# A hybrid recurrent decoder layer on one core: another centring for the layernorms, sums on VectorE, rows of 548 floats, and an alternating third merge

## The chip, the cores and the metric

The kernel runs on one core of a Trainium2 chip. Five engines work in parallel and each takes its own instructions in a fixed order: TensorE (PE in the profile; its weight loads are PEld), VectorE (DVE), ScalarE (ACT), GpSimd (POOL) and SyncE (SP), which here issues the loads of the weights. The metric is the device time of one execution in microseconds (us).

## The reference

One layer of a decoder is applied to 512 prompt tokens and to 8 x 4 sample tokens, 544 in all, with a model width of 1024:

```
proj   = x @ w_in + b_in
h_gla, h_ml, h_hg = three token mixers of parts of proj
gates  = sigmoid(mg).reshape(..., 3, 1024)
merged = gates[0]*(h_gla @ w_up_gla) + gates[1]*(h_ml @ w_up_ml) + gates[2]*(h_hg @ w_up_hg)
x = layernorm(alpha*x + merged @ w_out, ln1_g, ln1_b)
hid = square(relu(x @ w_ff_up))
x = layernorm(alpha*x + hid @ w_ff_down, ln2_g, ln2_b)
```

Outputs are x and the states of the mixers. All numbers are float32.

## The kernel before

Activations are held transposed: channels on the 128 partitions, the 544 tokens along a row, eight tiles of 128 channels (KD). A product of full precision is made of three: each operand is split into a high part and a rest (xh and xl of x, wh and wl of a weight tile), and high x high, high x rest and rest x high are summed. A gemm (L163) of one output tile with eight input tiles is therefore 8 x 3 x 2 = 48 matmuls, since the 544 tokens go in two halves of 272.

Weights come by `wload` (L133): a DMA into one of three buffers raw, ScalarE copies it into wh (L141), VectorE subtracts to get wl (L142). wh and wl have two buffers each, so the weights of a gemm can be split only when the gemm before the last has read its own. The PSUM results have two buffers too, and one is free again when VectorE has read it.

The stages follow one another: input projection and the three mixers, with gemms of the projection filling TensorE; three merges; output projection with the first layernorm; the FFN in two blocks of 16 hidden tiles; the second layernorm. Inside an engine a scheduler fixes the order at build time; `high_priority` draws weight splits and evacuations forward.

A **merge** (class at L839) takes a branch: `gates` computes four gate tiles (a gemm over x, L853 to add the bias, L206 to L208 for the sigmoid), `split` divides the branch's result into hh and hl, `products` makes four tiles of h @ w_up, multiplies them by their gates (L868) and adds them to `merged` on GpSimd (L872). The third merge, of the HGRN2 branch, has two input tiles, so that a product has 12 matmuls; it computes all eight gates first, then all eight products, and splits each finished tile of merged into mh and ml (L179, L180).

The **first layernorm** works on tiles as they leave the output projection (L1015 to L1020; L1019 adds alpha*x). `ln_tile` (L953) adds up tiles 0 to 3, takes the mean over those 512 channels by a matmul with ones5 (L967), and centres: tiles 0 to 3 in one go, later tiles as they come (L972). Of each centred tile ScalarE takes the square (L974), and GpSimd adds tile and square to the sums a1 and a2 (L978, L979); for the last tile VectorE does. `put_x1` (L1009) writes the FFN's operands x1h and x1l. `ln_sums` and `ln_end` turn the sums into ne (the negative mean) and rstd. The **second layernorm** uses the same `ln_tile` on six tiles (L1061); tiles 6 and 7 are treated in token halves at the end (L1077 to L1095), with their weights split into lh and ll (L1071). Then each half gets ne added, rstd multiplied and the affine step (L1096 to L1107). The lists ADDP, MULP and AFFD (L30) say which tiles GpSimd adds, GpSimd multiplies and VectorE scales; the rest is VectorE's and ScalarE's.

The operands xh, xl, x1h and x1l are tiles of [128, 8, TX] with TX = T + 2 = 546 floats per row; the two extra columns hold the layernorm's gain and bias for the first FFN gemms.

## Time and profile before

| | us |
|---|---|
| median of 3 runs | 968.91 |
| lowest and highest run | 965.64 and 971.26 |
| the profiled execution | 968.76 |
| its span, first to last instruction | 966.9 |
| mean granted TensorE clock over the span | 0.977 of full speed |

A row of the profile names the line, the engine, the operation, and what it writes and reads (`out<-in`, buffer numbers left out); x is a count. A wait is put down to the instruction that ended it. The granted clock is the share of TensorE's full clock that it was allowed to run at. Busy time of TensorE contains waiting inside its pipeline, so that the start-to-start distance of matmuls says more than the length of one record.

### The profile page before, as it was taken

To read this page: it belongs to the slowest core of one execution; us is meant where nothing else is said; L and a number is where in the kernel's file an instruction comes from. 1 tells how busy PE (TensorE), PEld (TensorE's weight loads), DVE (VectorE), ACT (ScalarE), POOL (GpSimd) and SP (SyncE) were. 2 spreads that over 40 slices of the span, in tenths; PEclk is the share of its full clock that TensorE was granted. 3 is DMA by queue.
4 is the path that set the end of the run, shared out by engine and by line. 5 is a ranking of instruction groups with operands and counts; after the bars stand their busy time and mean duration, and the time that the engine had idled before them with its cause. 6 is when DMAs were issued, how large, how long until landed. Compare 5 with 4: busy or idle time off the path is not lost.

```text
span 966.9 us, 17405 instructions
## 1 busy us (share of the span) xinstructions
PE 926.0 (96%) x7279; PEld 910.7 (94%) x7279; DVE 569.1 (59%) x877; ACT 404.5 (42%) x688; POOL 232.9 (24%) x210
## 2 busy tenths in 40 slices
PE   8999999799999999999989798999999999999795
PEld 7998999799999999999989798999999999999794
DVE  4895467866775676773565855553222455532836
ACT  4386223643555443545523356542111344521414
POOL 0311232643102435120235692000000000001722
PEclk9999999899999999999999899999999999999898
DMA  7321241022132112041144222222222222222202
GB/s 258 118 86 44 84 129 57 16 87 88 60 96 90 49 47 97 25 158 55 33 154 121 79 67 87 88 88 88 87 88 87 88 87 88 88 87 88 85 3 93
DMA packets 37598, 82.73 MB, mean 86 GB/s; under 512 B 12709, under 2 KB 18341, under 8 KB 37521
## 3 DMA queue, kind: packets, MB, share of 16 engines
q1 hardware_dynamic: 25072, 73.28, 23.3%
q10 hardware_dynamic: 12384, 8.33, 3.0%
q8 instruction: 57, 0.93, 0.4%
q14 instruction: 21, 0.16, 0.1%
q0 software_dynamic: 64, 0.02, 0.0%
HBM read 76.51 MB, written 5.09 MB: 84 GB/s over the span
## 4 chain that ended last, share of the span: by engine, by line
PE 86%; DVE 6%; POOL 3%; issue 2%; ACT 1%; DMA 1%; ACTq 0%; DVEq 0%
PE g L158 74%; PE g L83 3%; PE lv L401 2%; POOL merged L1050 2%; POOL merged L1049 1%; DVE wl L142 1%; DVE qe L393 1%; DVE merged L972 1%; PE o L458 1%; DVE x1l L1013 1%; PE oTm L760 1%; PE qkp L673 0%; PE oT L282 0%; DVE ml L180 0%; DMA fw<-in_wfirst 0%
## 5 line engine op out<-in xcount | busy, mean ns | idle before, releaser
L142 DVE TENSOR_TENSOR wl<-raw,wh 128x1024 fp32r<-128x1024 f32 (+2 forms) x139 | 168.4, 1212 | 152.4 <-ACT wh L141 149.6
L141 ACT ACTIVATE wh<-raw 128x1024 fp32r<-128x1024 f32 (+2 forms) x139 | 133.3, 959 | 277.0 <-PE g L158 258.8
L158 PE MATMUL g<-xh,wh 128*128 128x272 f32 x752 | 162.1, 295 | 0.0
L158 PE MATMUL g<-xh,wl 128*128 128x272 f32 x752 | 161.2, 293 | 0.0
L158 PE MATMUL g<-xl,wh 128*128 128x272 f32 x752 | 161.1, 294 | 0.0
L158 PEld LDWEIGHTS g<-xl,wh 128*128 128x128 f32 x752 | 120.8, 191 | 0.9 <-issue 0.5
L158 PEld LDWEIGHTS g<-xh,wh 128*128 128x128 f32 x752 | 121.0, 192 | 0.7 <-issue 0.2
L158 PEld LDWEIGHTS g<-xh,wl 128*128 128x128 f32 x752 | 121.1, 192 | 0.3
L158 PE MATMUL g<-x1h,wh 128*128 128x272 f32 (+1 forms) x512 | 107.1, 290 | 2.9 <-DVE relu L1036 2.9
L158 PE MATMUL g<-x1l,wh 128*128 128x272 f32 (+1 forms) x512 | 106.9, 290 | 0.0
L158 PE MATMUL g<-x1h,wl 128*128 128x272 f32 (+1 forms) x512 | 106.9, 290 | 0.0
L158 PEld LDWEIGHTS g<-x1h,wh 128*128 128x128 f32 x512 | 81.2, 189 | 3.3 <-DVE relu L1036 3.3
L158 PEld LDWEIGHTS g<-x1l,wh 128*128 128x128 f32 x512 | 81.5, 190 | 0.1
L158 PEld LDWEIGHTS g<-x1h,wl 128*128 128x128 f32 x512 | 80.8, 188 | 0.0
L961 POOL TENSOR_TENSOR a<-merged 128x544 f32<-128x544 f32 x2 | 4.8, 2421 | 295.6 <-ACT wh L141 284.3
L158 PE MATMUL g<-hidl,wh 128*128 128x272 f32 x280 | 58.1, 289 | 0.0
L158 PE MATMUL g<-hidh,wh 128*128 128x272 f32 x280 | 57.9, 288 | 0.0
L158 PE MATMUL g<-hidh,wl 128*128 128x272 f32 x280 | 57.8, 288 | 0.0
L1038 ACT ACTIVATE relu<-relu,gw 128x544 f32<-128x544 f32 x32 | 24.0, 750 | 77.2 <-DVE relu L1037 77.2
L872 POOL TENSOR_TENSOR merged<-merged,gb 128x544 f32<-128x544 f32 x16 | 26.8, 1678 | 86.8 <-ACT gb L207 47.8
L215 DVE TENSOR_SCALAR gb<-g,vec 128x544 f32<-128x544 f32 x24 | 18.8, 782 | 45.2 <-PE g L158 45.1
L158 PEld LDWEIGHTS g<-hidl,wh 128*128 128x128 f32 x280 | 44.0, 188 | 0.0
(405 smaller groups left out, 1863.3 us busy)
## 6 DMA issues: line engine op xcount, KB each, us to landing
raw<-in_wff SPq DMA_DIRECT2D x64, 512.0 KB, 3.6
raw<-in_win SPq DMA_DIRECT2D x47, 512.0 KB, 3.2
xr<-in_xT SPq DMA_DIRECT2D x16, 272.0 KB, 3.2
raw<-in_wout SPq DMA_DIRECT2D x8, 512.0 KB, 4.0
out_yT<-merged SPq DMA_DIRECT2D x8, 272.0 KB, 2.4
fw<-in_wfirst ACTq DMA_DIRECT2D x8, 256.0 KB, 5.4
raw<-in_wup_ml SPq DMA_DIRECT2D x8, 192.0 KB, 2.3
raw<-in_wup_gla SPq DMA_DIRECT2D x8, 192.0 KB, 2.4
```

The costliest lines, as they stand in the source:

```text
L83: nc.tensor.matmul(first_ps[i][hf], w[:, i * 128:(i + 1) * 128], a[:, k, hf * HT:(hf + 1) * HT], start=(k == 0 and n == 0), stop=(k == KD ...
L141: nc.scalar.activation(out=h[:, 0:n], in_=raw[:, 0:n], func=AF.Copy)
L142: nc.vector.tensor_tensor(out=l[:, 0:n], in0=raw[:, 0:n], in1=h[:, 0:n].bitcast(F32), op=ALU.subtract)
L158: nc.tensor.matmul(ps[:, hf, 0:w_], w, a(k)[:, hf * HT:hf * HT + w_], start=(k == 0 and s == 0), stop=(k == nk - 1 and s == 2))
L215: nc.vector.tensor_scalar(out, ps, vcol(col), XMIN, ALU.add, ALU.max)
L393: nc.vector.tensor_tensor(out=Q[s, :, p, 0:L // 2].rearrange("p a (n m) -> p a n m", m=m), in0=blk(qv)[s, :, :, m:2 * m], in1=Ev[s, :, :, ...
L401: nc.tensor.matmul(lv[0:R, o:o + 2 * H].rearrange("p (a b) -> p a b", a=2), Kv[:, p, c * R:(c + 1) * R], Q[:, p, :, c * H:(c + 1) * H], st ...
L458: nc.tensor.matmul(o[:, h * dv:(h + 1) * dv], at[:, c * 4 + h, :], vtok[:, cc, h * dv:(h + 1) * dv], start=(h == 0), stop=(cc == 0 and h = ...
L760: nc.tensor.matmul(oT[0:97, h * 32 + 4 * n:h * 32 + 4 * n + 4], Cs[:, n, :], qF[h][:, 4 * n:4 * n + 4], start=False, stop=(h == 3 and n == 7))
L872: eng.tensor_tensor(out=merged[:, m, :], in0=merged[:, m, :], in1=g, op=ALU.add)
L1038: nc.scalar.activation(out=r_, in_=r_, func=AF.Relu, bias=gw[:, 1:2])
L1050: nc.gpsimd.tensor_tensor(out=y, in0=y, in1=rstd, op=ALU.mult)
```

## The change

Three things change. **Rows**: TX becomes T + 4, 548 floats. **Layernorms**: the mean that is subtracted is that of the first column tile alone (128 channels, ones7, copied to ScalarE's a1r in L956); each tile is centred as it comes; the sums are all made on VectorE (L968, L969), and the first tile's square is written straight to a2; ADDP, MULP and AFFD are empty, so the last steps are VectorE's and ScalarE's alone. The variance is still corrected for what is left of the mean. **Third merge**: gate tile m + 1 is computed, then product m, and so on; the second pool of gate buffers, gb2, is gone.

```diff
-TX = T + 2
+TX = T + 4
-ADDP, MULP, AFFD = (5, 6, 7), (7,), (2, 5)
+ADDP, MULP, AFFD = (), (), ()
...
-        gb2s, gb2p = pool("gb2", 4)
...
-        mr_.gates(0, gbp)
-        mr_.gates(4, gb2p)
+        mr_.gates(0, gbp, 1)
         mr_.split()
-        mr_.products(0)
-        mr_.products(4)
-        gb2s.close()
+        for m in range(KD):
+            if m + 1 < KD:
+                mr_.gates(m + 1, gbp, 1)
+            mr_.products(m, 1)
...
-        def ln_tile(x, m, sl, last, after):
+        def ln_tile(x, m, sl, after):
             if m == 0:
-                return
-            if m < 4:
-                eng = nc.vector if m == 3 else nc.gpsimd
-                to = a1 if m < 3 else ftile("a1r").bitcast(F32R)
-                eng.tensor_tensor(out=to[:, sl], in0=(x[:, 0, sl] if m == 1 else a1[:, sl]), in1=x[:, m, sl], op=ALU.add)
-                if m < 3:
-                    return
+                xr_ = ftile("a1r").bitcast(F32R)
+                nc.scalar.activation(out=xr_[:, sl], in_=x[:, 0, sl], func=AF.Copy)
                 for hf in range(2):
                     ps = psr.tile([128, 512], F32, tag="r", name="mu")
                     s = slice(hf * HT, (hf + 1) * HT)
-                    nc.tensor.matmul(ps[:, 0:HT], ones5, to[:, s], start=True, stop=True)
+                    nc.tensor.matmul(ps[:, 0:HT], ones7, xr_[:, s], start=True, stop=True)
                     nc.scalar.activation(out=cm[:, s], in_=ps[:, 0:HT], func=AF.Copy)
-                nc.gpsimd.memset(a1, 0.0)
-                nc.gpsimd.memset(a2, 0.0)
-            for i in range(0 if m == 3 else m, m + 1):
-                nc.vector.tensor_tensor(out=x[:, i, sl], in0=x[:, i, sl], in1=cm[:, sl], op=ALU.subtract)
-                sq = ftile("sq")
-                nc.scalar.activation(out=sq[:, sl], in_=x[:, i, sl], func=AF.Square)
-                if after:
-                    after(i, sl)
-                eng = nc.vector if last else nc.gpsimd
-                eng.tensor_tensor(out=a1[:, sl], in0=a1[:, sl], in1=x[:, i, sl], op=ALU.add)
-                eng.tensor_tensor(out=a2[:, sl], in0=a2[:, sl], in1=sq[:, sl], op=ALU.add)
+            nc.vector.tensor_tensor(out=x[:, m, sl], in0=x[:, m, sl], in1=cm[:, sl], op=ALU.subtract)
+            sq = ftile("sq") if m else a2
+            nc.scalar.activation(out=sq[:, sl], in_=x[:, m, sl], func=AF.Square)
+            if after:
+                after(m, sl)
+            if m:
+                nc.vector.tensor_tensor(out=a1[:, sl], in0=x[:, 0, sl] if m == 1 else a1[:, sl], in1=x[:, m, sl], op=ALU.add)
+                nc.vector.tensor_tensor(out=a2[:, sl], in0=a2[:, sl], in1=sq[:, sl], op=ALU.add)
```

`gates` and `products` get a count `n`. Lines behind this function move up by ten: L1019 becomes L1009, L1013 becomes L1003, L1036 becomes L1026, L1049 becomes L1039, L1051 becomes L1041, L1060 becomes L1050, L1075 becomes L1065; in the function, L972 becomes L962, L978 and L979 become L968 and L969, L967 becomes L960.

What the scheduler makes of it stands in the order of VectorE's instructions. Among the third merge's products it was (gb is a gate tile, wl of 128x256 belongs to a product, wl of 128x1024 to a gemm of eight tiles):

```order
L868 TENSOR_TENSOR gb<-g,gb 128x544
L180 TENSOR_TENSOR ml<-merged,mh 128x544
L142 TENSOR_TENSOR wl<-raw,wh 128x256
L868 TENSOR_TENSOR gb<-g,gb 128x544
L180 TENSOR_TENSOR ml<-merged,mh 128x544
L142 TENSOR_TENSOR wl<-raw,wh 128x256
L180 TENSOR_TENSOR ml<-merged,mh 128x544
L868 TENSOR_TENSOR gb<-g,gb 128x544
```

and is now, in its middle and then at its end:

```order
L215 TENSOR_SCALAR gb<-g,vec 128x544
L142 TENSOR_TENSOR wl<-raw,wh 128x1024
L868 TENSOR_TENSOR gb<-g,gb 128x544
L142 TENSOR_TENSOR wl<-raw,wh 128x256
L180 TENSOR_TENSOR ml<-merged,mh 128x544
```

```order
L868 TENSOR_TENSOR gb<-g,gb 128x544
L142 TENSOR_TENSOR wl<-raw,wh 128x1024 x2
L868 TENSOR_TENSOR gb<-g,gb 128x544
L180 TENSOR_TENSOR ml<-merged,mh 128x544 x2
L1009 SCALAR_TENSOR_TENSOR merged<-xr,g 128x544
```

The gate's evacuation and the large weight split have moved in between the products; the last product's L868 stands behind two large splits.

In the first layernorm VectorE had, from the output projection's fourth tile on:

```order
L1019 SCALAR_TENSOR_TENSOR merged<-xr,g 128x544
L961 TENSOR_TENSOR a1r<-a_5672,merged 128x544
L142 TENSOR_TENSOR wl<-raw,wh 128x1024
L972 TENSOR_TENSOR merged<-merged,cm 128x544 x4
L1019 SCALAR_TENSOR_TENSOR merged<-xr,g 128x544
L142 TENSOR_TENSOR wl<-raw,wh 128x1024
L1013 SCALAR_TENSOR_TENSOR x1l<-merged,vec,x1h 128x544
L972 TENSOR_TENSOR merged<-merged,cm 128x544
L1013 SCALAR_TENSOR_TENSOR x1l<-merged,vec,x1h 128x544 x3
L1019 SCALAR_TENSOR_TENSOR merged<-xr,g 128x544
L1013 SCALAR_TENSOR_TENSOR x1l<-merged,vec,x1h 128x544
L142 TENSOR_TENSOR wl<-raw,wh 128x1024
```

and has now, from its second tile on (a_5668 and a_5669 are a1 and a2):

```order
L1009 SCALAR_TENSOR_TENSOR merged<-xr,g 128x544
L142 TENSOR_TENSOR wl<-raw,wh 128x1024
L962 TENSOR_TENSOR merged<-merged,cm 128x544 x2
L968 TENSOR_TENSOR a_5668<-merged 128x544
L1003 SCALAR_TENSOR_TENSOR x1l<-merged,vec,x1h 128x544
L969 TENSOR_TENSOR a_5669<-a_5669,sq 128x544
L1003 SCALAR_TENSOR_TENSOR x1l<-merged,vec,x1h 128x544
L1009 SCALAR_TENSOR_TENSOR merged<-xr,g 128x544
L142 TENSOR_TENSOR wl<-raw,wh 128x1024
L962 TENSOR_TENSOR merged<-merged,cm 128x544
L968 TENSOR_TENSOR a_5668<-a_5668,merged 128x544
L969 TENSOR_TENSOR a_5669<-a_5669,sq 128x544
```

The four centrings in one piece became two, at an earlier tile, and the two sums came in; per tile one weight split remains.

In the second layernorm VectorE had, from the fourth tile on (ll are the rests of the last two tiles' weights):

```order
L1060 TENSOR_TENSOR merged<-merged,g 128x544
L961 TENSOR_TENSOR a1r<-a_5672,merged 128x544
L142 TENSOR_TENSOR wl<-raw,wh 128x1024
L972 TENSOR_TENSOR merged<-merged,cm 128x544 x4
L1075 TENSOR_TENSOR merged<-merged,cm 128x544 x2
L180 TENSOR_TENSOR ll<-raw,lh 128x1024
L142 TENSOR_TENSOR wl<-raw,wh 128x1024
L1060 TENSOR_TENSOR merged<-merged,g 128x544
```

and has now, from the first tile on:

```order
L1050 TENSOR_TENSOR merged<-merged,g 128x544
L142 TENSOR_TENSOR wl<-raw,wh 128x1024
L962 TENSOR_TENSOR merged<-merged,cm 128x544
L1065 TENSOR_TENSOR merged<-merged,cm 128x544 x2
L142 TENSOR_TENSOR wl<-raw,wh 128x1024
L1050 TENSOR_TENSOR merged<-merged,g 128x544
L962 TENSOR_TENSOR merged<-merged,cm 128x544
L142 TENSOR_TENSOR wl<-raw,wh 128x1024
L968 TENSOR_TENSOR a_5668<-merged 128x544
L969 TENSOR_TENSOR a_5669<-a_5669,sq 128x544
```

Of the seven instructions between two weight splits three are left, and they stand at an earlier tile. The rows up to the third merge's second gate are the same in both kernels.

## The prediction

> **What bounds the kernel now.** I read the page first: busy times, then the chain that ended last.

> ```profile
> PE 926.0 (96%) x7279; PEld 910.7 (94%) x7279; DVE 569.1 (59%) x877; ACT 404.5 (42%) x688; POOL 232.9 (24%) x210
> PE 86%; DVE 6%; POOL 3%; issue 2%; ACT 1%; DMA 1%; ACTq 0%; DVEq 0%
> ```

> TensorE is the bound: its matmuls are 86% of the chain, and no edit removes one of the large ones. What can be gained is its waits. So the second view is TensorE's waits from 476 us to 956 us, that is, from the third merge's products to the last matmul (columns: total us, times, longest).

> ```profile
> PE g L158 <- DVE wl L142: 11.0, 5, 5.5
> PE g L158 <- DVE merged L1019: 3.8, 1, 3.8
> PE g L158 <- DVE relu L1036: 2.9, 2, 1.6
> PE g L158 <- DVE gb L868: 1.0, 1, 1.0
> ```

> All of them are on VectorE. The third view places them: busy time by stretch, with the granted clock as the third number from the end.

> ```profile
> 476.00:499.00 23.00, 17.84 (x122) 16.81 (x121) 19.70 (x22) 8.78 (x15) 12.05 (x9) 0.93 0.41 132
> 492.30:495.70 3.40, 3.40 (x17) 3.40 (x16) 3.40 (x4) 0.66 (x1) 1.97 (x2) 0.50 0.49 153
> 517.00:556.00 39.00, 33.72 (x245) 33.23 (x244) 33.54 (x29) 15.38 (x23) 25.09 (x15) 0.91 0.29 90
> 540.00:546.90 6.90, 5.77 (x25) 5.77 (x26) 6.08 (x6) 3.31 (x5) 3.69 (x3) 0.51 0.36 113
> 895.00:920.00 25.00, 19.48 (x134) 19.26 (x133) 22.44 (x16) 9.67 (x14) 18.97 (x11) 0.86 0.27 85
> 912.10:918.90 6.80, 5.91 (x26) 5.91 (x27) 6.76 (x6) 2.66 (x3) 6.07 (x3) 0.50 0.71 224
> ```

> TensorE is idle for 23.00 - 17.84 = 5.2 us around the third merge's products, 39.00 - 33.72 = 5.3 us in the first layernorm and 25.00 - 19.48 = 5.5 us in the second. After each, the granted clock falls to one half for a while. At half clock a pair of matmuls starts every 0.46 us:

> ```profile
> 492.63 0.66 PE L158 MATMUL g<-mh,wh 128*128 128x272 f32 x2
> 493.09 0.65 PE L158 MATMUL g<-ml,wh 128*128 128x272 f32 x2
> 429.91 40.22 PE g L158 x317
> 689.88 95.14 PE g L158 x754
> L158 PE MATMUL g<-hidh,wh 128*128 128x272 f32 x280 | 57.9, 288 | 0.0
> ```

> The two chain pieces below them give the pitch at full clock: 40.22/317 = 126.9 ns (operand xh) and 95.14/754 = 126.2 ns (hid tiles). So 0.228 us becomes 0.126 us, and 45% of the busy time at half clock is lost: 1.5 us of 3.40, 2.6 of 5.77, 2.7 of 5.91. A record lasts 0.288 us though the next matmul could start after 0.126, so each wait costs 0.16 us beyond the idle time. Of the waits four lie in the third merge, two in the first layernorm and one in the second, beside the two on relu. That makes the losses: third merge 5.2 + 4 waits x 0.16 + 1.5 = 7.3 us; first layernorm 5.3 + 2 x 0.16 + 2.6 = 8.2; second 5.5 + 0.16 + 2.7 = 8.4.

> Why VectorE is late is in its timeline beside GpSimd's:

> ```profile
> 530.91 1.88 DVE L972 TENSOR_TENSOR merged<-merged,cm 128x544 f32<-128x544 f32 x1
> 541.00 0.71 DVE L972 TENSOR_TENSOR merged<-merged,cm 128x544 f32<-128x544 f32 x1
> 532.17 1.85 POOL L978 TENSOR_TENSOR a<-a,merged 128x544 f32<-128x544 f32 x1
> 910.59 2.35 DVE L142 TENSOR_TENSOR wl<-raw,wh 128x1024 fp32r<-128x1024 f32 x1
> 551.84 1.21 DVE L142 TENSOR_TENSOR wl<-raw,wh 128x1024 fp32r<-128x1024 f32 x1
> 552.98 0.71 DVE L978 TENSOR_TENSOR a<-a,merged 128x544 f32<-128x544 f32 x1
> 554.25 0.77 DVE L1013 SCALAR_TENSOR_TENSOR x1l<-merged,vec,x1h 128x544 fp32r<-128x544 f32 x1
> 538.08 0.71 DVE L1019 SCALAR_TENSOR_TENSOR merged<-xr,g 128x544 f32<-128x544 f32 x1
> ```

> The same subtraction takes 0.71 us alone and 1.88 us while GpSimd's adds run; a weight split takes 1.21 us or 2.35 us. Before, four column tiles are centred in one burst while GpSimd adds, and the next weight split stands behind the burst.

> **The change part by part.** Durations are of the profiled execution, which took 968.76 us (span 966.9); the median of the runs is 968.91, so the sum stands for both.

> *First layernorm.* All of GpSimd's sums leave it. In the new order VectorE has per output gemm: one weight split 1.21, L1009 (L1019 before) 0.71, centring 0.71, the two sums 0.71 each (the row of L978) and L1003 0.77, together 4.8 us. The gemm is 48 matmuls x 0.126 = 6.05 us. GpSimd has nothing to do there, so the short durations hold, and the burst of four becomes two (tiles 0 and 1 behind the mean): a weight split waits for at most 0.71 + 2 x 0.71 + 0.71 x 2 + 2 x 0.77 = 5.1 us, under the gemm that covers it. Gain 8.2 us. The last tile's chain ends with x1l some 4.8 us after the last output gemm; the first FFN gemm needs it only at its last k, after 42 x 0.126 = 5.3 us. The mean's two matmuls now stand four matmuls into the third output gemm (L960), and their operand is complete about 2 us earlier, since the first gemm's end is evacuated while 27 matmuls of the second still run. If this cover were gone, each us late would be a us of TensorE.

> *Second layernorm.* There VectorE has 2 x 1.21 + 0.71 + 3 x 0.71 = 5.3 us per 12.1 us (96 matmuls), and the four splits into ll come on top, 1.21 each, over the last two tiles. The burst before a weight split is gone; L1065 still stands ahead of one, with L962 3 x 0.71 = 2.1 us, and that split is needed a gemm later. Gain 8.4 us.

> *Third merge.* The old order ends in eight products of 12 matmuls, 1.5 us each, that VectorE and GpSimd can't follow; alternated, a gate gemm of 6.05 us covers each product's add, split and next weights. But the wait has a new place. The gate gemm after next needs the weight buffer that the gate gemm before it has just left, with one product, 1.5 us, and its own first four matmuls, 0.5 us, as cover. The old gate gemms show the lag:

> ```profile
> 435.91 1.06 ACT L141 ACTIVATE wh<-raw 128x1024 fp32r<-128x1024 f32 x1 [2.91 <-PE g L158]
> 436.24 0.79 DVE L215 TENSOR_SCALAR gb<-g,vec 128x544 f32<-128x544 f32 x1 [4.06 <-PE g L158]
> 437.00 1.23 DVE L142 TENSOR_TENSOR wl<-raw,wh 128x1024 fp32r<-128x1024 f32 x1
> 488.95 2.35 DVE L142 TENSOR_TENSOR wl<-raw,wh 128x1024 fp32r<-128x1024 f32 x1
> ```

> From the end of the gemm (436.2) to the end of its successor's split (438.23) are 2.0 us. The product starts 0.16 us before that end, so TensorE wants the split at +1.84 and waits about 0.25 us, seven times: 1.8 us. GpSimd's add is queued behind that split on VectorE, so it doesn't overlap it. At the end two weight splits for the output gemm stand ahead of the last L868, and the first overlaps GpSimd's add of tile 6: between 1.21 and 2.35 us (last row); I take the middle, and TensorE waits 0.9 us. Net 7.3 - 1.8 - 0.9 = 4.6 us; ends: 7.3 with no such wait, and 7.3 - 7 x (0.25 + 2.35 - 1.23) - 0.9 = -3.2 with every split at the long duration.

> In this term 1.5 us is the half clock from 492.3 on. The trace shows it behind one wait of 2.1 us. [...]

> *Rows of 548 floats.* Rows of 2184 bytes become 2192, so that every row of xh, xl, x1h and x1l starts at a multiple of 16 bytes as the hid tiles' do. The nearest rows are the two pitches: 126.9 against 126.2 ns, 0.7 ns on 2448 matmuls of xh and xl (47 gemms of 48, and 192 in the first block) is 1.7 us, which I take; the ends are 0 (the pitches differ for another cause) and 2.8 us (the 1536 of x1h and x1l gain too). [...] No row here separates odd rows from even ones.

> *Start of the FFN.* The two waits on relu (2.9 us) stay: GpSimd still scales x1 in one piece,

> ```profile
> 558.65 14.02 POOL L1049 TENSOR_TENSOR merged<-merged,ne 128x544 f32<-128x544 f32 x8
> 572.63 14.56 POOL L1050 TENSOR_TENSOR merged<-merged,rstd 128x544 f32<-128x544 f32 x8
> ```

> and ScalarE's order around L1041 is as before. Taken at nothing; ends 0 and a gain of 3.2.

> *The tail.* Adds, products and affines of the last half leave GpSimd and VectorE's L1105:

> ```profile
> 955.59 4.02 DVE L1099 TENSOR_TENSOR merged<-merged,ne 128x272 f32<-128x272 f32 x5
> 959.53 2.54 DVE L1103 TENSOR_TENSOR merged<-merged,rstd 128x272 f32<-128x272 f32 x7
> 960.00 3.14 ACT L1107 ACTIVATE merged<-merged,vec 128x272 f32<-128x272 f32 x6 [3.31 <-DVE merged L1103]
> ```

> Eight adds at the short pitch, 2.54/7 = 0.36 us, take 2.9 us instead of 4.0; the first product starts 1.1 us earlier, but ScalarE then has eight affines at 3.14/6 = 0.52 us, 4.2 us instead of 3.1. The last one ends where it did. Nothing.

> Sum: 8.2 + 8.4 + 4.6 + 1.7 = 22.9 us, so 968.8 - 22.9 = 945.9, say **946 us**.

> **The rivals.** (1) Long splits in the alternation: if GpSimd's add falls on the weight split in each period, the third merge is at its lower end, 7.8 us worse: 954 us. For it speaks that the overlap did double that split at 488.95; against it that L868, which releases the add, stands behind the split.

> (2) VectorE becomes the bound, and the kernel slower than before: the doubling isn't GpSimd's doing but comes from ScalarE reading the same tiles. Then each output gemm has 2.35 + 0.71 + 4 x 1.88 = 10.6 us of VectorE against 6.05 us, 4.5 us late eight times, 36 us: 982 us. It decides from 6.05 us on, and the change loses outright above 6.05 + 22.9/8 = 8.9 us per gemm. For it speaks that VectorE was busy 33.54 of 39 us there; against it the 0.71 us at 552.98, when GpSimd was idle. [...]

> (3) The mean comes late: L960 waits in TensorE's queue behind an evacuation, a copy on ScalarE and a weight split, 0.71 + 0.56 (544 of the 1024 columns that take L141 1.06 us) + 1.21 = 2.5 us in each layernorm: 951 us.

> (4) The change doesn't do what it says: the waits were set by the order of the weight loads alone, and reappear with the clock drops. Then about 965 to 970 us.

> **How the numbers follow.** Forecast 0.70; (1) 0.09; (2) 0.04; (3) 0.06; (4) 0.05; better than the forecast's range, with the FFN's waits gone too, 0.06. Low end: no alternation wait (2.7), 2.8 us of alignment instead of 1.7 (1.1), relu waits gone (3.2) and the runs' spread, 968.91 - 965.64 = 3.3: 936. High end: rival (1) with no gain from alignment, 954 + 1.7, rounded up: 956. Outside are (2), (4) and part of the better case. A measurement tells 0.5% from no change, 4.8 us. Faster by more than that: 0.70 + 0.09 + 0.06 + 0.06 and a little of (4) = 0.92; the same 0.04; slower 0.04.

> **What would show it.** Right: L962, L968 and L969 at 0.71 us and no wait of TensorE in the output projection and the second layernorm; granted clock 1.00 from the third merge to the last matmul; about 0.25 us of wait for wl L142 before each gate gemm from the third on; the two relu waits still there; xh's pitch at 126.2 ns. Wrong: two-input VectorE operations near 1.9 us with GpSimd idle; waits of over 1 us in the alternation; a wait at L960; the clock at 0.50 again.

## The result and the profile after

| | before | after |
|---|---|---|
| median of 4 runs, us | 967.27 | 943.11 |
| lowest and highest | 965.32 to 971.26 | 941.76 to 943.46 |
| the profiled execution, its span | 968.76, 966.9 | 943.46, 941.4 |
| mean granted clock | 0.977 | 0.985 |

The ratio is 0.9742 (95% interval 0.9706 to 0.9779): 24 us less, 946 was forecast. The page of the changed kernel, busy times and the shares of its chain by engine:

```profile
PE 915.9 (97%) x7279; PEld 900.1 (96%) x7279; DVE 553.3 (59%) x901; ACT 407.1 (43%) x694; POOL 166.4 (18%) x168
PE 83%; DVE 6%; POOL 4%; ACT 3%; DMA 2%; issue 1%; ACTq 0%; POOLq 0%; SPq 0%; DVEq 0%
```

VectorE is as busy as before (59%) though it took over the sums: its instructions became shorter (the mean of L962's is 0.72 us, that of L972's was 1.23). TensorE's waits from the third merge to the last matmul (total us, times, longest), then busy time by stretch in the third merge, at the start of the output projection, in the first and in the second layernorm:

```profile
PE g L158 <- DVE relu L1026: 3.1, 2, 1.6
PE g L158 <- DVE wl L142: 2.4, 7, 1.4
434.00:476.00 42.00, 41.04 (x316) 39.71 (x315) 20.68 (x28) 21.59 (x35) 7.00 (x5) 1.00 0.21 69
476.00:499.00 23.00, 21.57 (x172) 21.35 (x171) 11.46 (x16) 9.27 (x15) 4.46 (x3) 1.00 0.43 134
505.00:544.00 39.00, 39.00 (x306) 38.68 (x305) 27.91 (x38) 15.59 (x24) 0.18 (x1) 1.00 0.36 110
880.00:905.00 25.00, 25.00 (x201) 25.00 (x200) 14.42 (x18) 8.01 (x9) 0.00 (x0) 1.00 0.26 85
```

18.7 us of waits have become 5.5. In both layernorms TensorE is busy all the time (39.00 of 39.00, 25.00 of 25.00) and the granted clock is 1.00 in every stretch. VectorE's timeline in the first layernorm shows four consecutive instructions of the new order, each at its short duration:

```profile
505.48 1.23 DVE L142 TENSOR_TENSOR wl<-raw,wh 128x1024 fp32r<-128x1024 f32 x1 [0.17 <-ACT wh L141]
506.62 0.72 DVE L962 TENSOR_TENSOR merged<-merged,cm 128x544 f32<-128x544 f32 x1
507.37 0.72 DVE L968 TENSOR_TENSOR a<-a,merged 128x544 f32<-128x544 f32 x1
508.06 0.73 DVE L969 TENSOR_TENSOR a<-a,sq 128x544 f32<-128x544 f32 x1
```

What is left stands in the chain of waits (start, us, what): a short wait in each period of the third merge, and the start of the output projection.

```profile
433.45 1.07 ACT wh L141
434.55 1.24 DVE wl L142
435.83 5.56 PE g L158 x42
...
482.89 1.05 ACT wh L141
483.97 2.39 DVE wl L142
486.40 3.68 PE g L158 x27
```

Six times a gate gemm waits for its weight split. Once, after the matmul that starts at 484.68, TensorE waits for a split of 2.39 us; beside that split runs GpSimd's add of tile 6:

```profile
483.90 1.36 POOL L872 TENSOR_TENSOR merged<-merged,gb 128x544 f32<-128x544 f32 x1 [6.11 <-DVE gb L868]
```

By the distance between starts, which adds 0.16 us to each idle time as in the prediction, these waits are 6 x 0.32 and 1.6 us.

The two traces are cut where a stage's first matmul starts (the first cut is the split of the third merge's operand, L865). The columns are us in the profiled execution.

| stretch | before | after | less |
|---|---|---|---|
| up to the third merge | 424.49 | 422.16 | 2.3 |
| third merge | 64.13 | 62.15 | 2.0 |
| output projection, first layernorm | 60.69 | 50.20 | 10.5 |
| FFN, first block up | 102.88 | 102.25 | 0.6 |
| first block down | 96.41 | 96.42 | 0.0 |
| second block up | 97.70 | 96.75 | 0.95 |
| second block down, second layernorm | 80.99 | 72.58 | 8.4 |
| last gemms and tail | 39.57 | 38.86 | 0.7 |

The 10.5 us hold 1.5 us of the half clock that followed the old third merge, and 0.65 us that the wait at the first output gemm is shorter (2.24 before, 1.6 now); the rest, 8.3, is the first layernorm. The 2.3 us of the first row can't be given to the rows alone: up to there m_only and s_vector (below) run the code of the kernel before, with rows of 546, and they get there at 422.41 and 420.82 where the kernel before took 424.49.

### The profile page after: what moved, and what is told of

The parts are those of the page before. It is cut to its first block, busy times and chain, and to the rows that moved or that the text cites. A ratio compares the mean times of both kernels' runs of the same rounds, so it can differ in the third digit from the quotient of the medians.

```text
span 941.4 us, 17347 instructions
## 1 busy us (share of the span) xinstructions
PE 915.9 (97%) x7279; PEld 900.1 (96%) x7279; DVE 553.3 (59%) x901; ACT 407.1 (43%) x694; POOL 166.4 (18%) x168
## 4 chain that ended last, share of the span: by engine, by line
PE 83%; DVE 6%; POOL 4%; ACT 3%; DMA 2%; issue 1%; ACTq 0%; POOLq 0%; SPq 0%; DVEq 0%
PE g L158 73%; PE lv L401 3%; DVE wl L142 2%; POOL merged L1040 1%; ACT wh L141 1%; POOL merged L1039 1%; DMA xr<-in_xT 1%; DVE qe L393 1%; PE o L458 1%; POOL cvo L583 1%; PE oTm L760 1%; DMA Cs<-in_mC 1%; PE qkp L673 0%; PE oT L282 0%; DMA raw<-in_win 0%
## 5 line engine op out<-in xcount | busy, mean ns | idle before, releaser
L142 DVE TENSOR_TENSOR wl<-raw,wh 128x1024 fp32r<-128x1024 f32 (+2 forms) x139 | 163.4, 1176 | 142.8 <-ACT wh L141 140.4
L141 ACT ACTIVATE wh<-raw 128x1024 fp32r<-128x1024 f32 (+2 forms) x139 | 133.3, 959 | 261.0 <-PE g L158 225.3
L158 PE MATMUL g<-xh,wl 128*128 128x272 f32 x752 | 161.5, 294 | 1.1 <-DVE wl L142 1.1
L158 PE MATMUL g<-xh,wh 128*128 128x272 f32 x752 | 160.6, 293 | 0.0
L158 PE MATMUL g<-xl,wh 128*128 128x272 f32 x752 | 160.2, 292 | 0.0
L158 PEld LDWEIGHTS g<-xh,wl 128*128 128x128 f32 x752 | 119.9, 190 | 3.0 <-DVE wl L142 2.7
L158 PEld LDWEIGHTS g<-xh,wh 128*128 128x128 f32 x752 | 120.5, 191 | 0.7 <-issue 0.4
L158 PEld LDWEIGHTS g<-xl,wh 128*128 128x128 f32 x752 | 120.0, 191 | 0.9 <-issue 0.5
L158 PE MATMUL g<-x1h,wh 128*128 128x272 f32 (+1 forms) x512 | 106.5, 289 | 3.1 <-DVE relu L1026 3.1
L158 PE MATMUL g<-x1l,wh 128*128 128x272 f32 (+1 forms) x512 | 106.7, 289 | 0.0
L158 PE MATMUL g<-x1h,wl 128*128 128x272 f32 (+1 forms) x512 | 106.0, 288 | 0.0
L158 PEld LDWEIGHTS g<-x1h,wh 128*128 128x128 f32 x512 | 80.8, 189 | 3.6 <-DVE relu L1026 3.6
L158 PEld LDWEIGHTS g<-x1l,wh 128*128 128x128 f32 x512 | 81.5, 190 | 0.1
L158 PEld LDWEIGHTS g<-x1h,wl 128*128 128x128 f32 x512 | 81.0, 188 | 0.0
L158 PE MATMUL g<-hidh,wh 128*128 128x272 f32 x280 | 58.1, 288 | 0.0
L158 PE MATMUL g<-hidl,wh 128*128 128x272 f32 x280 | 58.1, 289 | 0.0
L158 PE MATMUL g<-hidh,wl 128*128 128x272 f32 x280 | 57.8, 288 | 0.0
L158 PEld LDWEIGHTS g<-hidl,wh 128*128 128x128 f32 x280 | 44.0, 188 | 0.0
L158 PEld LDWEIGHTS g<-hidh,wl 128*128 128x128 f32 x280 | 43.9, 188 | 0.0
L158 PEld LDWEIGHTS g<-hidh,wh 128*128 128x128 f32 x280 | 43.8, 188 | 0.0
L872 POOL TENSOR_TENSOR merged<-merged,gb 128x544 f32<-128x544 f32 x16 | 25.7, 1611 | 86.2 <-DVE gb L868 83.1
```

The lines of the kernel that those rows point to most:

```text
L141: nc.scalar.activation(out=h[:, 0:n], in_=raw[:, 0:n], func=AF.Copy)
L142: nc.vector.tensor_tensor(out=l[:, 0:n], in0=raw[:, 0:n], in1=h[:, 0:n].bitcast(F32), op=ALU.subtract)
L158: nc.tensor.matmul(ps[:, hf, 0:w_], w, a(k)[:, hf * HT:hf * HT + w_], start=(k == 0 and s == 0), stop=(k == nk - 1 and s == 2))
L872: eng.tensor_tensor(out=merged[:, m, :], in0=merged[:, m, :], in1=g, op=ALU.add)
```

## The experiments

Times are medians in us; the ratio is to the kernel before, run on the same chip in the same group.

| label | kernel | time | before | ratio (95%) |
|---|---|---|---|---|
| r_same | the changed kernel again | 944.56 | 966.85 | 0.9767 (0.9745 to 0.9789) |
| r_after546 | changed, rows of 546 | 946.21 | 966.85 | 0.9782 (0.9759 to 0.9805) |
| r_after550 | changed, rows of 550 | 946.55 | 966.85 | 0.9778 (0.9754 to 0.9802) |
| r_before548 | before, rows of 548 | 961.34 | 966.85 | 0.9941 (0.9924 to 0.9959) |
| m_only | before, alternating merge | 961.92 | 966.71 | 0.9946 (0.9919 to 0.9973) |
| m_undone | changed, old merge | 945.33 | 966.71 | 0.9779 (0.9757 to 0.9801) |
| s_gpsimd | changed, sums on GpSimd | 944.58 | 966.71 | 0.9768 (0.9748 to 0.9788) |
| s_vector | before, sums on VectorE | 957.34 | 966.71 | 0.9894 (0.9859 to 0.9928) |
| e_lastadds | changed, last adds on VectorE | 943.84 | 969.18 | 0.9745 (0.9724 to 0.9765) |
| e_ownbufs | changed, product weights apart | 940.21 | 969.18 | 0.9705 (0.9684 to 0.9725) |
| e_scale | changed, x1 scaled on VectorE | 943.84 | 969.18 | 0.9741 (0.9721 to 0.9762) |
| e_best | the two edits above together | 939.59 | 969.18 | 0.9699 (0.968 to 0.9718) |

The changed kernel's own medians, 943.11 and 944.56, show what a comparison across groups resolves: about 1.5 us.

### The rows

```diff
-TX = T + 4
+TX = T + 2
```

This is r_after546; r_after550 has T + 6, and r_before548 is the kernel before with T + 4.

> The changed kernel itself, as the base of this group: 943 us, and matmul pitches of 125.7 ns on xh and 126.0 ns on x1h.

> The changed kernel with rows of 546 floats, as before the change. Theory: the rows that don't start at a multiple of 16 bytes cost their matmuls about 1 ns each, so the pitch on xh and x1h goes back to about 127 ns and the time to 943 + 4 = 947 us. Rival (the term of the prediction): 1.7 us at most, 945 us; second rival: the pitch has nothing to do with the rows, 943 us.

> The changed kernel with rows of 550 floats: longer than 548 as 548 is longer than 546, but odd rows are off a multiple of 16 bytes by 8 again. Theory (16 bytes count): the same as with 546, about 947 us and 127 ns. Rival (the length of the rows, or another placement of the tiles, is what counts, not the 16 bytes): 943 us and 125.7 ns, as with 548.

> The kernel before with rows of 548 floats and nothing else changed. Theory: pitches of 125.7 to 126 ns on xh and x1h, and about 4 us off, 963 us. Rival: 1.7 us off, 965.5 us, or nothing.

Each kernel's chain has a piece of 239 matmuls, most of them on xh and xl, at full clock. In this order: before, changed, changed with 546, changed with 550, before with 548 (start, us, what):

```profile
280.27 30.30 PE g L158 x239
278.40 30.01 PE g L158 x239
279.27 30.30 PE g L158 x239
280.74 30.28 PE g L158 x239
278.26 30.01 PE g L158 x239
```

And the long piece in the FFN, for the changed kernel, with 546 and with 550:

```profile
577.40 270.61 PE g L158 x2149
577.90 272.15 PE g L158 x2149
578.32 271.79 PE g L158 x2149
```

Rows of 546 and of 550 floats cost the same, rows of 548 are shorter by 1.2 ns a matmul (0.29 us of 239): among these three sizes the multiple of 16 bytes counts and not the length. The start-to-start distances, sorted by row, show where: with 550, matmuls on odd rows of xh and xl (which start 8 bytes off) take 127.3 and 128.0 ns for the two halves, on even rows 125.6; with 548 the four numbers lie between 125.4 and 126.0. Over all matmuls the distances of r_after546 add up to 1.8 us (xh, xl) and 1.9 us (x1h, x1l) more than those of r_same, 3.7 us. The times give 1.7 and 2.0 us in the changed kernel, hardly more than the 1.5 us by which the changed kernel's own medians differ, and 5.5 in the kernel before (its interval is 4 to 7). Part of the 5.5 may be chance: in the profile of r_before548 the wait at the first output gemm is the same (2.25 us, 2.24 before), but no half clock follows it, which is 1.5 us. By the measured times the size stays open between 1.7 and 5.5 us; by the distances it is 3.7.

### The layernorms

In s_gpsimd the new mean and the new order stay, and only the sums go back (but for the last tile's). In s_vector the old mean and its burst of four centrings stay, and only the sums move.

```diff
-                nc.vector.tensor_tensor(out=a1[:, sl], in0=x[:, 0, sl] if m == 1 else a1[:, sl], in1=x[:, m, sl], op=ALU.add)
-                nc.vector.tensor_tensor(out=a2[:, sl], in0=a2[:, sl], in1=sq[:, sl], op=ALU.add)
+                eng = nc.vector if m == KD - 1 else nc.gpsimd
+                eng.tensor_tensor(out=a1[:, sl], in0=x[:, 0, sl] if m == 1 else a1[:, sl], in1=x[:, m, sl], op=ALU.add)
+                eng.tensor_tensor(out=a2[:, sl], in0=a2[:, sl], in1=sq[:, sl], op=ALU.add)
```

```diff
-                eng = nc.vector if m == 3 else nc.gpsimd
+                eng = nc.vector
...
-                eng = nc.vector if last else nc.gpsimd
+                eng = nc.vector
```

> The changed kernel with the sums of the layernorms on GpSimd for all tiles but the last, as before; the mean of the first tile stays. Theory (GpSimd's adds double VectorE's two-input operations, and that makes the waits): centring and weight splits at 1.9 and 2.35 us beside the adds, waits and half clock back in part, most of the 16.6 us lost, about 953 to 958 us. Rival (the burst of four centrings at one place made the waits): the doubling is seen, but a single centring per gemm leaves room, and the time stays within 2 us of 943 us.

> The kernel before with the sums of the layernorms on VectorE; the mean over four tiles and the burst of four centrings stay, and so does the first merge order. Theory (GpSimd's adds): the burst takes 4 x 0.71 us and not 4 x 1.88, most of the layernorms' 16.6 us gained, 952 to 956 us. Rival (the burst): VectorE now has the eight sums of the burst as well, 4 x 0.71 + 8 x 0.71 = 8.5 us at one place before the next weight split, the waits and clock drops stay, 965 us or more.

My theory failed in the first: s_gpsimd lost nothing (944.58 beside 944.56). Its waits are those of the changed kernel,

```profile
PE g L158 <- DVE relu L1027: 3.2, 2, 1.6
PE g L158 <- DVE wl L142: 2.4, 7, 1.4
```

and from the third merge's split to the end it takes 519.18 us where r_same takes 519.19. VectorE's timeline and GpSimd's (below) in its first layernorm show why:

```profile
512.94 0.73 DVE L962 TENSOR_TENSOR merged<-merged,cm 128x544 f32<-128x544 f32 x1
513.59 1.22 DVE L142 TENSOR_TENSOR wl<-raw,wh 128x1024 fp32r<-128x1024 f32 x1
515.04 1.57 DVE L1004 SCALAR_TENSOR_TENSOR x1l<-merged,vec,x1h 128x544 fp32r<-128x544 f32 x1 [0.23 <-ACT x1h L1003]
...
513.81 2.21 POOL L969 TENSOR_TENSOR a<-a,merged 128x544 f32<-128x544 f32 x1 [0.94 <-DVE merged L962]
515.98 1.85 POOL L970 TENSOR_TENSOR a<-a,sq 128x544 f32<-128x544 f32 x1
```

The split started 0.22 us ahead of GpSimd's sum and kept its 1.22 us; the sum took 2.21 instead of 1.36. Then x1l started while that sum ran until 516.02, and was done 0.59 us after it. So this is no general doubling: here the two engines took turns. What came second ended 1.21 us (the sum, 1.36 alone) and 0.59 us (x1l, 0.79 alone) after the other: most of its own length lay behind the other's end. The kernel before shows the same, by these two rows of GpSimd:

```profile
530.37 1.84 POOL L979 TENSOR_TENSOR a<-a,sq 128x544 f32<-128x544 f32 x1
537.54 1.81 POOL L979 TENSOR_TENSOR a<-a,sq 128x544 f32<-128x544 f32 x1
```

The subtraction that the prediction quotes at 530.91 (1.88 us) ended 0.58 us after the first of them; L1019 at 538.08, inside the second, took its 0.71, as did L1019 at 526.80, inside an earlier sum (526.26, 1.83 us). One operand of L1019, g, lies in PSUM; the instructions that took a turn in these rows read two tiles in SBUF. That this is what sets them apart is my reading; no run varied it alone.

A single centring per gemm therefore cost VectorE one turn here, 1.57 instead of 0.79 us for x1l, with 6.05 us of gemm to spend. In the kernel before, four centrings released eight sums at once; GpSimd ran them back to back, some 1.8 us each, and for 15 us (523.19 to 538.16) every VectorE instruction with two SBUF inputs took 1.75 to 1.89 us: it waited a turn.

s_vector is the other half. The second layernorm has no wait, and the first has none from the second output gemm to the last, although the burst is there. Its row in s_vector, and in the kernel before:

```profile
518.26 2.63 DVE L972 TENSOR_TENSOR merged<-merged,cm 128x544 f32<-128x544 f32 x4 [2.49 <-ACT cm L968]
521.91 4.97 DVE L972 TENSOR_TENSOR merged<-merged,cm 128x544 f32<-128x544 f32 x4 [2.42 <-ACT cm L968]
```

It now lasts 2.63 us. The 4.97 us before were not 4 x 1.88, as my expectation has it: GpSimd's first sum started at 522.78, so that only the third and fourth centring waited a turn. s_vector's waits hold a new one of 2.9 us at the start of the FFN instead (relu, a split ahead of it on VectorE), with half clock behind it (one of the eleven drops of the last section):

```profile
PE g L158 <- DVE relu L1036: 4.5, 3, 2.9
PE g L158 <- DVE wl L142: 4.0, 3, 2.1
PE g L158 <- DVE gb L868: 1.0, 1, 1.0
```

The trace shows where that split is held up: it waits for ScalarE's copy at 551.07, which stands in ScalarE's order behind the end of the layernorm, and that waits for the matmuls of the sums (L985). They start at 548.51, 11.2 us after the first FFN matmul; in the changed kernel (L975) it is 6.2 us. Why they stand so late was not followed. 957.34 lies 1.3 us above the range of the theory. Its runs spread from 952.82 to 958.68, and the trace is of the one of 952.82: what the others lose beyond it is not shown.

So each of the two cures takes away the waits inside the layernorms by itself, and the loss there needed both: the burst and the turns.

### The third merge

> The kernel before with the alternating third merge alone. Theory: the waits among the products and the half clock behind them go (7.3 us), six or seven waits of 0.3 us and one of about 1.6 us at the start of the output projection come in, net about 4 us: 963 us; the layernorms' waits and clock drops stay. Rival: the alternation is worth nothing by itself, since its splits are late in another place: 967 us.

> The changed kernel with the third merge as before (all gates, then all products). Theory: the waits of some 5 us among the products and the half clock behind them come back, 943 + 4 = 947 us; no wait in the layernorms. Rival: with the first layernorm no longer waiting, the merge's lag is taken up later and nothing is lost: 943 us.

m_only is the diff's part on the third merge alone, m_undone all the rest of it. m_only gains 4.8 us. In the changed kernel the same edit is worth less: 945.33 without it, 943.11 and 944.56 with it; from the merge's split to the first FFN matmul 114.44 us without and 112.36 with, 2.1 us (the medians alone, 0.8 and 2.2 us apart, don't settle it). The waits of m_undone:

```profile
PE g L158 <- DVE wl L142: 4.0, 3, 2.1
PE g L158 <- DVE relu L1027: 3.1, 2, 1.6
PE g L158 <- DVE gb L868: 1.0, 1, 1.0
```

The old merge's waits are back (by distances 1.12, 1.14, 0.25, 1.20 and 2.25, together 5.95 us, against 6 x 0.32 + 1.6 = 3.5; the wait of 0.25 is too short for the rows above). But no half clock follows them; in the stretch from 476 to 499 the clock is 1.00, where the kernel before had 0.93:

```profile
476.00:499.00 23.00, 17.86 (x134) 16.81 (x133) 19.20 (x20) 8.61 (x13) 8.85 (x6) 1.00 0.46 135
```

The rest of m_only's gain is half clock. From the first output gemm to the first FFN matmul m_only takes 57.41 us where the kernel before takes 60.69. Of these 3.28 us, 1.5 are the half clock behind the old merge and 0.65 the wait at the first output gemm; 1.1 are left. The waits of the old first layernorm are nearly the same (5.76 and 5.87 us by distances), but its 6.8 us of half clock start at another point of them, so that 18 matmuls run in it and not 25, which is 1.0 us.

### The waits that were left

```diff
-                    eng = nc.gpsimd
+                    eng = nc.vector if self.fin and m >= KD - 2 else nc.gpsimd
...
-                h, l = wload(src, n)
+                h, l = wload(src, n, pw)
...
-                    nc.gpsimd.tensor_tensor(out=y, in0=y, in1=ne, op=ALU.add)
-                    nc.gpsimd.tensor_tensor(out=y, in0=y, in1=rstd, op=ALU.mult)
+                    nc.vector.tensor_tensor(out=y, in0=y, in1=ne, op=ALU.add)
+                    nc.vector.tensor_tensor(out=y, in0=y, in1=rstd, op=ALU.mult)
```

The three pieces are e_lastadds, e_ownbufs (pw is a pool with two buffers of 256 columns each for wh and wl of the third merge's products; `wload` takes its tiles from it) and e_scale; e_best has the second and the third.

> The changed kernel with the adds to merged (L872) of the third merge's last two tiles on VectorE, so that GpSimd does nothing at the start of the output projection. Theory: the weight split there took 2.39 us because it had to let GpSimd's add of tile 6 finish first; alone it takes 1.21, and the wait of 1.6 us falls to some 0.4 to 0.9 us (VectorE makes the adds itself, 0.71 each): time 1 us lower, about 943. Rival: the wait is set by the order on VectorE and by the two splits that stand there, 2 x 1.21, and stays at 1.6 us or grows.

> The changed kernel with small weight buffers of their own for the third merge's products, so that a gate gemm's weights can be split two gemms earlier. Theory: the six waits of 0.32 us and the one of 1.6 us at the start of the output projection were the price of the two shared buffers and go, 3.5 us: about 940 to 941 us. Rival: VectorE's order, not the buffers, sets them: no difference, 944 us.

> The changed kernel with the scaling of x1 during the FFN's first block (L1039, L1040) on VectorE instead of GpSimd. Theory: the two waits on relu (1.85 us each) come from VectorE's relu steps that have to let GpSimd's long adds finish first, and go: 3.4 us less, about 940.5 us. Rival: VectorE gets 16 more instructions of 0.7 us there and is late at another gemm: no gain or a loss.

> Both of the last two edits. Theory: their gains add, 7 us: 937 us, with TensorE waiting nowhere from the third merge to the last matmul. Rival: one wait hid another, and the sum is less, 940 us.

In e_lastadds the two splits at the start of the output projection take 2.35 us together,

```profile
483.59 0.72 DVE L872 TENSOR_TENSOR merged<-merged,gb 128x544 f32<-128x544 f32 x1
484.24 2.35 DVE L142 TENSOR_TENSOR wl<-raw,wh 128x1024 fp32r<-128x1024 f32 x2
```

where the first alone took 2.39: the turn that GpSimd's add took there is shown. The wait falls from 1.6 to 0.87 us, too little to be seen in the time. e_ownbufs removes all seven waits; of TensorE's waits one row is left (its line numbers are four to six higher):

```profile
PE g L162 <- DVE relu L1032: 3.2, 2, 1.6
```

It is 2.9 to 4.4 us faster than the changed kernel's two medians, which come from other groups, and 3.6 us faster than e_lastadds and e_scale in its own; 3.5 was the sum of the waits. e_scale gains nothing. Its two relu waits are gone, but a wait of 2.2 us stands ahead of them; in e_best, which has it too, VectorE's timeline shows what made it (the last row is the busy time of the stretch from 540 to 551):

```profile
539.68 5.17 DVE L1045 TENSOR_TENSOR merged<-merged,ne 128x544 f32<-128x544 f32 x8 [0.16 <-ACT ne L992]
544.77 1.22 DVE L146 TENSOR_TENSOR wl<-raw,wh 128x1024 fp32r<-128x1024 f32 x1
545.90 0.77 DVE L1032 SCALAR_TENSOR_TENSOR relu<-ne,gw,g 128x544 f32<-128x544 f32 x1
540.00:551.00 11.00, 8.76 (x60) 8.54 (x60) 11.00 (x17) 6.59 (x12) 0.00 (x0) 0.87 0.17 49
```

All eight adds become ready at once, when ne is, and the scheduler put them ahead of the first relu: a burst again, and half clock behind it (0.87 in the last row). So the gains did not add; e_best (939.59) can't be told from e_ownbufs (940.21). Both beat the changed kernel, by 2.9 us or more.

## Why the prediction came out as it did

- **Layernorms, 8.2 and 8.4 us**: 8.3 and 8.4. The sizes were right, and the cause was half right. The prediction named both, the burst and GpSimd's adds beside it. "GpSimd has nothing to do there, so the short durations hold" is what the trace shows, but it wasn't needed: s_gpsimd has the same time. What counted was that the burst met an engine that took turns with VectorE (a centring took 1.88 us beside GpSimd's sums, 0.71 alone); ending either was enough.
- **Third merge, 4.6 us**: in the profiled pair 2.0 + 0.65 + 1.5 = 4.1, with some 0.4 of the rows' gain in it. Within it, "0.25 us, seven times" was six times 0.32, 1.9 for 1.8. "I take the middle" at the start of the output projection failed: 0.9 forecast, 1.6 measured, since the split waited for the whole add. And the 1.5 us of half clock was not the merge's own: m_undone has the waits without it, so the edit by itself is worth 2.1 us. That the term came out near 4.6 is partly luck: the drop was in the profiled execution.
- **Rows, 1.7 us**: too small. The distances say 3.7 us. In the profiled pair 0.6 + 0.95 us lie in the FFN's stretches on x1h and x1l, which only the rows touch, and 0.4 in the merge; the 2.3 up to the third merge hold the rest, but that stretch varies from run to run by as much (it ends at 423.39 in r_same, 1.2 us later than in the profiled run of the changed kernel). The step took 0.7 ns from one piece each of xh and hid, for xh and xl alone, while the odd rows alone cost 1.7 ns and more in xh and xl, and x1h and x1l gained as much. The end at 2.8 us was too low as well.
- **Start of the FFN, nothing**: right, 3.1 us of waits are there (2.9 before).
- **Tail, nothing**: 0.7 us less, from 12.1 after the last matmul to 11.4. Up to the last affine step it was as worked out (ScalarE's eight took 4.14 us, forecast 4.2); the rest lies behind it and was not followed.
- **Sum**: 22.9 forecast, 25.3 in the profiled execution. The 2.4 us more are 2.0 for the rows (by the distances) and 0.7 for the tail, less 0.9 of the merge; the 0.6 that remain are within what the first stretch varies by. The total came out closer than its terms, since the rows' miss and the merge's lie on opposite sides.
- **Rivals**: (1) the splits in the alternation took 1.24 us, not 2.35; it holds at one place only, the start of the output projection. (2) VectorE's two-input rows are at 0.72 us with ScalarE reading the same tiles. (3) No wait for the mean at L960. (4) The layernorms' waits and clock drops are gone.

## What to carry to other kernels

VectorE, busy 59% of the time, made TensorE wait 18.7 us in the kernel before: look for the place where one event (a mean, a sum, an rstd) makes many instructions ready at once, and at what stands behind them in the same engine's order. Before moving work off GpSimd, ask which of its instructions actually overlap a VectorE instruction with two SBUF inputs on the path (here 1.75 to 1.89 us beside GpSimd's sums, 0.71 to 1.21 alone); in these layernorms spreading them out did by itself as much as spreading and moving them together. Count a half clock behind a wait of some 2 us as chance: behind the old merge's wait of 2.2 us it came in two of four profiles.

## What the runs showed of the hardware

**Rows off 16 bytes cost about 1.7 to 2.4 ns of 126 ns a matmul** (r_after550: 127.3 and 128.0 ns on odd rows of xh and xl, 125.6 on even ones). On x1h and x1l the sums show a cost of the same size (1.9 us), but single rows don't separate so cleanly: in r_after550 the two halves take 125.4 and 129.0 ns on odd rows, 127.0 and 126.4 on even ones.
